# The recurrent block of layer one with its block-diagonal products behind the next tile's first product, and an out projection in half blocks

## The chip, the cores and the metric

The kernel runs on one core of a Trainium2 chip. The metric is the time of one execution on the device in microseconds (us), the median of several runs. The engines are called by the profile's names: PE is TensorE (PEld its weight loads), DVE is VectorE, ACT is ScalarE, POOL is GpSimd, and SP issues most of the DMAs.

## What is computed

The program is two blocks of a language model on 1024 tokens of width 1024, in float32. The first block has two layers: a recurrent layer ("hawk") with its feed-forward part, and an RWKV-7 layer with its own. The second block mixes a state-space layer and windowed attention. The change touches the recurrent layer alone. Cut to what matters it is:

```python
def hawk_block(x, w_in, b_in, conv_w, conv_b, wa, ba, wx, bx, lam, w_out, b_out):
    gx = x @ w_in + b_in                                  # 1024 -> 2 x 1280
    gate_branch, rec_branch = jnp.split(gx, 2, axis=-1)
    gate_branch = jax.nn.gelu(gate_branch)
    rec = causal_depthwise_conv(rec_branch, conv_w, conv_b)   # width 4
    rec = rg_lru(rec, wa, ba, wx, bx, lam)
    return (rec * gate_branch) @ w_out + b_out            # 1280 -> 1024

def rg_lru(x, wa, ba, wx, bx, lam):
    r = jax.nn.sigmoid(block_diag_linear(x, wa, ba))      # 10 blocks of 128 x 128
    i = jax.nn.sigmoid(block_diag_linear(x, wx, bx))
    log_a = -LRU_C * r * jax.nn.softplus(-lam)
    a = jnp.exp(log_a)
    b = jnp.sqrt(-jnp.expm1(2.0 * log_a)) * (i * x)
    ...  # h[t] = a[t] h[t-1] + b[t], along the tokens
    return h
```

## The kernel before, in words

Activations are held transposed, a channel tile of 128 rows by 512 tokens; the 1024 tokens are two halves. A float32 product is made from high and low fp32r parts: `mm3` (L191 to L193) issues three matmuls for each 128 rows of depth, high by high, high by low and low by high. So one output tile of depth 1024 is 24 matmuls. The weights come as a stream in a fixed order (class `Weights`): an SP load into one of two raw buffers, an ACT cast to the high part (L60, `whi`), a DVE difference for the low part (L65, `wlo`), into one of three split buffers. Products go to six rotating PSUM buffers (`mm`); two more (`aux`) serve small products.

The recurrent layer goes through ten channel tiles j of the inner width 1280, a step each, and then a step 10 without a new tile. In step j:

- `bd_gates(j-1)`: twelve matmuls, the two block-diagonal products of the tile before for both halves. They read `hxh` and `hxl`, the split conv output (L196 ACT, L197 DVE). ACT reads the four PSUM tiles (L414, L415: `hr`, `hi`), POOL multiplies (L416), ACT goes on to a tanh (L419).
- `rec(j, 0)`: the product of the recurrent branch for half 0 (24 matmuls, weight `hrec`); DVE takes it out of PSUM (L376, `hR`), makes the conv in four DVE operations (L379 once, L383 three times, `hX`), and splits it.
- `bd_decay(j-1)`: ACT exp and square (L424, L425), a DVE step (L426, `hb`), ACT square root (L429), a POOL product (L431).
- `rec(j, 1)`: the same for half 1.
- `bd_scan(j-1)` for each half: the recurrence as one DVE scan (L437), then POOL's product with the gate (L441).
- `gate(j)` for both halves: 48 matmuls with the weight `hgate`; DVE takes each out of PSUM (L394, `hG`), ACT makes the gelu (L395).
- `bd_split(j-1)`: the split of the gated result (`y`, L196 and L197).
- `outp`: in steps 3, 5, 7 and twice in 10 a block of two channel tiles goes through the out projection: 16 output tiles of six matmuls each, added to the residual `h` by DVE (L463/464 or L263). The last block also starts the next norm: an ACT and a DVE operation make the norm's split input (`hgh` L223, `hgl` L224), and ACT and POOL add squares.

The program order is that of the text above, but a scheduler with a model of the engines sets the order of each engine's instructions. It is a list for each engine; an instruction that waits holds up everything behind it on its engine. The feed-forward part that follows has the weight stream's next tiles, and the preparation of the second block (`s5_prep`, L1240 and on) is interleaved with it.

Of the kernel before, what the change touches and what calls it, by code (L numbers as in the profile page):

```python
# [28 lines left out]
class Weights:  # L29
    """Streams weight tiles in a fixed order: load, then split into two fp32r parts."""  # L30
# [23 lines left out]
    def _split(self, i):  # L54
# [6 lines left out]
        if kp < 128:                  # copies of 32 rows: (high, high, low) in one operand  # L61
            s = (slice(64, 96), s[1])
            self.nc.vector.tensor_tensor(out=hi[s], in0=t[s], in1=f32(hi[s]), op=SUB)
        else:
            self.nc.vector.tensor_tensor(out=lo[s], in0=t[s], in1=f32(hi[s]), op=SUB)  # L65
# [30 lines left out]
class Kernel:  # L96
# [4 lines left out]
    # ---------------------------------------------------------------- set-up  # L101
# [76 lines left out]
    # ------------------------------------------------------------ primitives  # L178
# [5 lines left out]
    def mm3(self, ps, w, x, nk, kofs=0, start=True, stop=True, kp=128, m=128):  # L184
        """ps += W^T x over nk row tiles; w = (hi, lo), x(k) -> (hi, lo)."""
# [13 lines left out]
    def split3(self, out, src, q):  # L199
        """out = three copies of 32 rows, high parts but for copy q, which has the low ones."""  # L200
# [4 lines left out]
    # norm whose 1/rms is applied after the product it feeds  # L205
# [6 lines left out]
    def norm_add(self, s, k, half, h=None):  # L212
        """h[k][half] is final: split gain*h, and add its squares."""
# [51 lines left out]
    # ----------------------------------------------------------------- start  # L265
    def load_x(self, yp):
        """x transposed to h, and its norm begun; x waits in tiles that the layer needs later."""
# [33 lines left out]
    # ------------------------------------------------------------------ hawk  # L301
    def hawk_weights(self):
# [3 lines left out]
        for j in range(10):  # L306
# [3 lines left out]
            for b in self.HB:  # L310
                if b[2] == j:
                    self._hawk_out_weights(w_out, b)
        for b in self.HB:
            if b[2] == 10:
                self._hawk_out_weights(w_out, b)

    def _hawk_out_weights(self, w_out, b):
        for q in range(2):
            self.W.add(("hout", b[0], q), [(0, 2, w_out[:, b[0]:b[1], q * 512:(q + 1) * 512])], 128, 2, 512)

    # channel tiles [a, b) go through the out projection after tile c's products
    HB = ((0, 2, 3), (2, 4, 5), (4, 6, 7), (6, 8, 10), (8, 10, 10))

    def hawk_consts(self, pool):
        """c = -8 softplus(-lambda), through log1p(u) = 2 atanh(u / (2 + u)), and the conv's bias."""
# [28 lines left out]
    def hawk(self, yp):  # L354
# [8 lines left out]
        def rec(j, half, w):  # L363
            p = self.psum()
# [5 lines left out]
            # the bias comes in with the conv's, so the padding is its negative  # L370
# [5 lines left out]
            tt(out=R[:, 3:], in0=p, in1=n0["rstd"][half], op=MUL)  # L376
            X = ht("hX", 2)
# [9 lines left out]
            st[j, half] = {"R": R, "X": X, "xs": (xh, xl)}  # L387
# [63 lines left out]
        def outp(b):  # L451
            a, e, _ = b
            last = e == 10
            for m in range(8):
                if m % 4 == 0:
                    wq = self.W.get(("hout", a, m // 4))
                w = tuple(t[:, :, (m % 4) * 128:(m % 4 + 1) * 128] for t in wq)
                for half in range(2):
                    p = self.psum()
                    self.mm3(p, w, lambda k: self.y[a + k, half], e - a)  # L460
                    self.run_deferred()
                    h = self.h[m, half]
                    if a == 0:  # L463
                        nc.vector.scalar_tensor_tensor(out=h, in0=p, scalar=self.v("lru_b_out", m), in1=h,
                                                       op0=ADD, op1=ADD)
                    else:
                        self.add_h(m, half, p)
# [1613 lines left out]
```

## Time and profile before

| | us |
|---|---|
| three runs | 3677.23, 3682.78, 3699.7 |
| their median | 3682.78 |
| the profiled execution, its span | 3682.5 |
| PE busy | 3477.9 (94% of the span) |
| DVE busy | 2453.6 (67%) |
| ACT busy | 1546.1 (42%) |
| POOL busy | 766.1 (21%) |

For the profiled execution nothing but its span is recorded, and the span lies 0.3 us under the median of the runs. The recurrent layer takes the first 465 us of the span. PE is the engine to look at: its idle time and the stretches at a lower granted clock are what a change of order can win. In the profile's timelines a row has its start, its length, the engine, the source line, the operation with output and inputs, how many rows it stands for, and in brackets the idle time ahead of it with what ended that.

### The profile page before, as it was taken

How to read it: one execution, taken by the hardware profiler on the slowest of the kernel's cores; microseconds unless marked ns; L12 is line 12 of the kernel's file. 1: busy time of each engine (PE TensorE's matmuls, PEld its weight loads, DVE VectorE, ACT ScalarE, POOL GpSimd, SP SyncE). 2: the span in 40 equal slices, each digit the busy share in tenths (PEclk: the TensorE clock that was granted, in tenths of full speed). 3: DMA queues.
4: the chain of work that ended last, by engine and by line, in shares of the span. 5: the costliest groups of instructions: out<-in, count | busy, mean ns of one | idle time of the engine just before them, and what ended most of it. 6: DMA issues, size and time to landing. Idle time of an engine off the chain costs nothing.

```text
span 3682.5 us, 49614 instructions
## 1 busy us (share of the span) xinstructions
PE 3477.9 (94%) x18603; PEld 2788.9 (76%) x18603; DVE 2453.6 (67%) x4254; ACT 1546.1 (42%) x2318; POOL 766.1 (21%) x1194
## 2 busy tenths in 40 slices
PE   7999899999999989999899899999999999799999
PEld 5777677777777867888678678887888888577777
DVE  7666778877675598467845985466544476886764
ACT  5665632223434452234444632334322254158553
POOL 4222358830210040012300410002000023240020
PEclk8999899999999989899899899999999999899999
DMA  3111113333443474732544646325323222121533
GB/s 98 42 41 38 35 47 94 106 107 110 119 124 118 134 214 110 163 91 80 171 123 143 199 135 157 100 70 152 92 83 112 64 86 85 55 90 49 184 90 113
DMA packets 626289, 388.86 MB, mean 106 GB/s; under 512 B 100212, under 2 KB 578208, under 8 KB 626048
## 3 DMA queue, kind: packets, MB, share of 16 engines
q1 hardware_dynamic: 619152, 373.07, 35.0%
q0 software_dynamic: 2944, 8.48, 0.7%
q10 hardware_dynamic: 3952, 4.13, 0.4%
q8 instruction: 147, 2.41, 0.3%
q14 instruction: 94, 0.77, 0.1%
HBM read 317.25 MB, written 68.35 MB: 105 GB/s over the span
## 4 chain that ended last, share of the span: by engine, by line
PE 43%; DVE 11%; DMA 3%; issue 3%; ACT 2%; SPq 1%; POOL 0%; DVEq 0%; ACTq 0%; POOLq 0%
PE mm L191 10%; PE mm L193 10%; PE mm L192 10%; DVE wlo L65 2%; PE g L1031 1%; DVE U L1562 1%; PE zy L1073 1%; PE g L1080 1%; PE zy L1070 1%; PE zy L1106 1%; DVE lnP L947 1%; PE mm L1773 1%; PE mm L1771 1%; PE mm L1772 1%; DVE lnT L949 1%
## 5 line engine op out<-in xcount | busy, mean ns | idle before, releaser
L191 PE MATMUL mm<-hgh,whi 128*128 128x512 f32 x2272 | 910.6, 401 | 13.4 <-DVE U L1562 9.9
L192 PE MATMUL mm<-hgl,whi 128*128 128x512 f32 x2272 | 904.6, 398 | 6.2 <-DVE hgl L224 6.2
L193 PE MATMUL mm<-hgh,wlo 128*128 128x512 f32 x2272 | 901.4, 397 | 5.2 <-DVE wlo L65 4.0
L60 ACT CAST whi<-wr 128x1024 fp32r<-128x1024 f32 (+3 forms) x566 | 478.4, 848 | 1014.4 <-PE mm L192 626.3
L65 DVE TENSOR_TENSOR wlo<-wr,whi 128x1024 fp32r<-128x1024 f32 (+3 forms) x564 | 571.3, 1014 | 290.7 <-ACT whi L60 271.1
L191 PEld LDWEIGHTS mm<-hgh,whi 128*128 128x128 f32 x2272 | 435.5, 192 | 114.6 <-issue 18.8
L193 PEld LDWEIGHTS mm<-hgh,wlo 128*128 128x128 f32 x2272 | 434.3, 191 | 102.8 <-DVE wlo L65 9.0
L192 PEld LDWEIGHTS mm<-hgl,whi 128*128 128x128 f32 x2272 | 435.3, 192 | 100.2 <-DVE hgl L224 7.5
L238 POOL TENSOR_TENSOR acc<-acc,sq 128x512 f32<-128x512 f32 x84 | 132.5, 1582 | 773.0 <-ACT sq L237 386.7
L193 PE MATMUL mm<-mh,wlo 128*128 128x512 f32 x704 | 277.0, 400 | 13.0 <-DVE wlo L65 12.3
L191 PE MATMUL mm<-mh,whi 128*128 128x512 f32 x704 | 279.0, 405 | 10.2 <-ACT whi L60 3.7
L192 PE MATMUL mm<-ml,whi 128*128 128x512 f32 x704 | 279.9, 398 | 1.6 <-DVE ml L197 1.5
L547 DVE TENSOR_TENSOR f<-mm,rstd 128x512 f32<-128x512 f32 x176 | 120.4, 685 | 235.6 <-PE mm L193 235.2
L263 DVE TENSOR_TENSOR h<-mm,h 128x512 f32<-128x512 f32 x272 | 182.3, 682 | 87.1 <-PE mm L193 86.4
L193 PEld LDWEIGHTS mm<-mh,wlo 128*128 128x128 f32 x704 | 134.5, 191 | 49.5 <-DVE wlo L65 20.5
L191 PEld LDWEIGHTS mm<-mh,whi 128*128 128x128 f32 x704 | 134.7, 192 | 47.9 <-ACT whi L60 9.5
L192 PEld LDWEIGHTS mm<-ml,whi 128*128 128x128 f32 x704 | 134.7, 191 | 30.2 <-DVE ml L197 3.2
L196 ACT CAST mh<-f 128x512 fp32r<-128x512 f32 x88 | 54.6, 621 | 199.4 <-DVE f L552 199.4
L880 POOL TENSOR_TENSOR t_s<-t_c,t_s 128x512 f32<-128x512 f32 x16 | 23.6, 1478 | 518.8 <-DVE t_c L878 518.8
L192 PE MATMUL mm<-xl,whi 128*128 128x512 f32 (+2 forms) x320 | 127.4, 400 | 0.0
L193 PE MATMUL mm<-xh,wlo 128*128 128x512 f32 (+2 forms) x320 | 126.9, 399 | 0.4 <-DVE wlo L65 0.3
L191 PE MATMUL mm<-xh,whi 128*128 128x512 f32 (+2 forms) x320 | 123.7, 398 | 3.4 <-DVE h L263 2.1
(617 smaller groups left out, 6294.2 us busy)
## 6 DMA issues: line engine op xcount, KB each, us to landing
wr<-in_ffn_w_in_dram SPq DMA_DIRECT2D x162, 512.0 KB, 3.8
wr<-in_ffn_w_out_dram SPq DMA_DIRECT2D x120, 256.0 KB, 2.8
wr<-in_rw_w_rkv_dram SPq DMA_DIRECT2D x48, 512.0 KB, 3.8
wr<-in_ple_w_gate_dram SPq DMA_DIRECT2D x24, 512.0 KB, 3.9
wr<-in_ffn_w_out_dram SPq DMA_DIRECT2D x56, 192.0 KB, 2.5
wr<-in_lru_w_in_dram SPq DMA_DIRECT2D x20, 512.0 KB, 3.8
wr<-in_w_in_dram SPq DMA_DIRECT2D x18, 512.0 KB, 4.4
hD<-h SPq DMA_DIRECT2D x32, 256.0 KB, 2.6
```

The source lines that it names most:

```text
L60: self.nc.scalar.copy(out=hi[s], in_=t[s])
L65: self.nc.vector.tensor_tensor(out=lo[s], in0=t[s], in1=f32(hi[s]), op=SUB)
L191: mm(ps, a, xh, start=start and k == 0, stop=False)
L192: mm(ps, a, xl, start=False, stop=False)
L193: mm(ps, b, xh, start=False, stop=stop and k == nk - 1)
L196: self.nc.scalar.copy(out=hi, in_=src)
L238: nc.gpsimd.tensor_tensor(out=a, in0=a, in1=q, op=ADD)
L263: self.nc.vector.tensor_tensor(out=h, in0=ps, in1=h, op=ADD)
L547: tt(out=t, in0=p, in1=nin["rstd"][half], op=MUL)
L947: nc.vector.tensor_tensor(out=p, in0=N[:, s, s + 1:32].unsqueeze(2).to_broadcast([128, r, c]), in1=X[:, s:s + 1, 0:c].to_broadcast([128, r ...
L949: nc.vector.tensor_tensor(out=X[:, s + 1:32, 0:c], in0=X[:, s + 1:32, 0:c], in1=p, op=ADD)
L1031: mm(p[e][:, q * 128:(q + 1) * 128], s["KB"][r, 4 * g + q, :], s["AR"][r, 4 * g + q, :], start=True, stop=True)
```

## The change

In step j the product of the recurrent branch for half 0 now stands ahead of the block-diagonal products of the tile before, so `rec` is cut into `rec_product` and `rec_conv`; the conv steps are issued after the products that follow on PE. The out projection's first three blocks are cut in two by output rows: after the gate products of steps 3 to 8 one half block of eight output tiles runs (one weight tile of 512 columns), where steps 3, 5 and 7 had sixteen. It now stands ahead of `bd_split`. The blocks of step 10 stand as (6, 8) before the last split and (8, 10) after it, and the last one goes by token halves: eight output tiles of half 0, its norm, then eight of half 1. Other hunks remove comments only; line numbers behind L300 move by up to 19.

```diff
@@ -307,22 +307,19 @@
             c = DR + j * 128
             W.add(("hrec", j), [(0, 8, w_in[:, :, c:c + 128])], 128, 8, 128)
             W.add(("hgate", j), [(0, 8, w_in[:, :, j * 128:(j + 1) * 128])], 128, 8, 128)
-            for b in self.HB:
-                if b[2] == j:
-                    self._hawk_out_weights(w_out, b)
-        for b in self.HB:
-            if b[2] == 10:
-                self._hawk_out_weights(w_out, b)
-
-    def _hawk_out_weights(self, w_out, b):
-        for q in range(2):
-            self.W.add(("hout", b[0], q), [(0, 2, w_out[:, b[0]:b[1], q * 512:(q + 1) * 512])], 128, 2, 512)
-
-    # channel tiles [a, b) go through the out projection after tile c's products
-    HB = ((0, 2, 3), (2, 4, 5), (4, 6, 7), (6, 8, 10), (8, 10, 10))
+            self._hawk_out_weights(w_out, j)
+        self._hawk_out_weights(w_out, 10)
+
+    def _hawk_out_weights(self, w_out, j):
+        for a, q in self.HO.get(j, ()):
+            self.W.add(("hout", a, q), [(0, 2, w_out[:, a:a + 2, q * 512:(q + 1) * 512])], 128, 2, 512)
+
+
+    HO = {3: ((0, 0),), 4: ((0, 1),), 5: ((2, 0),), 6: ((2, 1),), 7: ((4, 0),), 8: ((4, 1),),
+          10: ((6, 0), (6, 1), (8, 0), (8, 1))}
...
@@ -361,19 +358,27 @@
         st = {}
         self.y = {}
         def rec(j, half, w):
+            rec_product(j, half, w)
+            rec_conv(j, half)
+
+        def rec_product(j, half, w):
             p = self.psum()
             self.mm3(p, w, self.xof(n0, half), 8)
             self.run_deferred()
             if j == 0 and half == 0:
                 self.hawk_consts(yp)
             R = ht("hR", 2, n=HALF + 3)
+
             if half == 0:
                 nc.vector.tensor_scalar(out=R[:, 0:3], in0=self.ones[:, 0:3], scalar1=self.v("lru_b_in", 10 + j),
                                         scalar2=-1.0, op0=MUL, op1=MUL)
             else:
                 nc.vector.tensor_copy(out=R[:, 0:3], in_=st[j, 0]["R"][:, HALF:HALF + 3])
             tt(out=R[:, 3:], in0=p, in1=n0["rstd"][half], op=MUL)
+            st[j, half] = {"R": R}
+
+        def rec_conv(j, half):
+            R = st[j, half]["R"]
             X = ht("hX", 2)
             cw = self.vcol["lru_conv_w"]
             nc.vector.tensor_scalar(out=X, in0=R[:, 0:HALF], scalar1=self.vecs[:, cw + j:cw + j + 1],
@@ -384,7 +389,7 @@
                                                in1=X, op0=MUL, op1=ADD)
             xh, xl = ht("hxh", 2, F32R), ht("hxl", 2, F32R)
             self.split(xh, xl, X)
-            st[j, half] = {"R": R, "X": X, "xs": (xh, xl)}
+            st[j, half].update(X=X, xs=(xh, xl))
@@ -448,28 +453,35 @@
             self.split(yh, yl, st[j, half]["i"])
             self.y[j, half] = (yh, yl)
 
-        def outp(b):
-            a, e, _ = b
-            last = e == 10
-            for m in range(8):
-                if m % 4 == 0:
-                    wq = self.W.get(("hout", a, m // 4))
-                w = tuple(t[:, :, (m % 4) * 128:(m % 4 + 1) * 128] for t in wq)
+        def out_rows(a, m, half, w):
+
+            p = self.psum()
+            self.mm3(p, w, lambda k: self.y[a + k, half], 2)
+            self.run_deferred()
+            h = self.h[m, half]
+            if a == 0:
+                nc.vector.scalar_tensor_tensor(out=h, in0=p, scalar=self.v("lru_b_out", m), in1=h,
+                                               op0=ADD, op1=ADD)
+            else:
+                self.add_h(m, half, p)
+
+        def outp(a, q):
+            wq = self.W.get(("hout", a, q))
+            for m in range(4):
+                w = tuple(t[:, :, m * 128:(m + 1) * 128] for t in wq)
                 for half in range(2):
-                    p = self.psum()
-                    self.mm3(p, w, lambda k: self.y[a + k, half], e - a)
-                    self.run_deferred()
-                    h = self.h[m, half]
-                    if a == 0:
-                        nc.vector.scalar_tensor_tensor(out=h, in0=p, scalar=self.v("lru_b_out", m), in1=h,
-                                                       op0=ADD, op1=ADD)
-                    else:
-                        self.add_h(m, half, p)
-                    if last:
-                        self.norm_add(self.n1, m, half)
-                        if m == 7:
-                            self.norm_done(self.n1, half)
+                    out_rows(a, 4 * q + m, half, w)
                     yield
+
+        def out_last(a):
+            wq = [self.W.get(("hout", a, q)) for q in range(2)]
+            for half in range(2):
+                for m in range(8):
+                    w = tuple(t[:, :, (m % 4) * 128:(m % 4 + 1) * 128] for t in wq[m // 4])
+                    out_rows(a, m, half, w)
+                    self.norm_add(self.n1, m, half)
+                    yield
+                self.norm_done(self.n1, half)
 
@@ -478,7 +490,7 @@
             if j < 10:
                 w = self.W.get(("hrec", j))
             if j == 0:
...
@@ -486,13 +498,17 @@
                 rec(0, 1, w)
                 gate(0, 1, wg)
             if j:
+                if j < 10:
+                    rec_product(j, 0, w)
+                    yield
                 bd_gates(j - 1, wbd)
                 if j < 10:
-                    rec(j, 0, w)
+                    rec_conv(j, 0)
+                    rec_product(j, 1, w)
                 yield
                 bd_decay(j - 1)
                 if j < 10:
-                    rec(j, 1, w)
+                    rec_conv(j, 1)
                 yield
                 for half in range(2):
                     bd_scan(j - 1, half)
@@ -503,17 +519,20 @@
                 for half in range(2):
                     gate(j, half, w)
                     yield
+            if j < 10:
+                for a, q in self.HO.get(j, ()):
+                    yield from outp(a, q)
+            else:
+                self.n1 = self.norm_begin(self.hg, lambda k: self.v("norm_ffn", k))
+                yield from outp(6, 0)
+                yield from outp(6, 1)
             if j:
                 for half in range(2):
                     bd_split(j - 1, half)
-            for b in self.HB:
-                if b[2] == j:
-                    if b[1] == 10:
-                        self.n1 = self.norm_begin(self.hg, lambda k: self.v("norm_ffn", k))
-                    yield from outp(b)
-
-    # ------------------------------------------------------------------- ffn
-    # blocks of the inner width for one half at a time, then for both
+        yield from out_last(8)
+
```

In the built program the same operations stand on each engine, but for twelve ACT table loads fewer. Three places show what moved. In the names a number at the end tells buffers of one name apart.

First PE at step 3, where the block-diagonal products of tile 2 are taken up (`hxh_898` is half 0's operand, `hxh_945` half 1's; `mm_996` is the last gate product of step 2). Before:

```order
L193 MATMUL mm_996<-hgh_486,wlo_828 128x512
L191 MATMUL mm_1038<-hxh_898,wbh_958 128x512
L192 MATMUL mm_1038<-hxl_899,wbh_958 128x512
L193 MATMUL mm_1038<-hxh_898,wbl_959 128x512
L191 MATMUL mm_1039<-hxh_898,wbh_958 128x512
L192 MATMUL mm_1039<-hxl_899,wbh_958 128x512
L193 MATMUL mm_1039<-hxh_898,wbl_959 128x512
L191 MATMUL mm_1053<-hxh_945,wbh_958 128x512
L191 MATMUL mm_1054<-hxh_945,wbh_958 128x512
L191 MATMUL mm_1070<-hgh_184,whi_962 128x512
L192 MATMUL mm_1070<-hgl_185,whi_962 128x512
L192 MATMUL mm_1053<-hxl_946,wbh_958 128x512
```

In the change (`whi_962` is the weight of step 3's recurrent product):

```order
L191 MATMUL mm_1038<-hgh_285,whi_962 128x512
L192 MATMUL mm_1038<-hgl_286,whi_962 128x512
L193 MATMUL mm_1038<-hgh_285,wlo_963 128x512
L191 MATMUL mm_1066<-hxh_898,wbh_958 128x512
L192 MATMUL mm_1066<-hxl_899,wbh_958 128x512
L193 MATMUL mm_1066<-hxh_898,wbl_959 128x512
L191 MATMUL mm_1067<-hxh_898,wbh_958 128x512
L192 MATMUL mm_1067<-hxl_899,wbh_958 128x512
L193 MATMUL mm_1067<-hxh_898,wbl_959 128x512
L191 MATMUL mm_1081<-hxh_945,wbh_958 128x512
```

All 24 matmuls of `mm_1038`, the recurrent product of step 3, now stand between the gate product and the block-diagonal ones, and half 1's products come in one piece.

Second DVE in step 4, from the decay steps to the scans (`hb_1409` before and `hb_1367` in the change are the second half's). Before:

```order
L426 SCALAR_TENSOR_TENSOR hb_1409<-hr_1406,hb_1409 128x512
L376 TENSOR_TENSOR hR_1440<-mm_1415,rstd0_331 128x512
L437 SCALAR_TENSOR_TENSOR hi_1392<-ha_1393,hi_1392 128x512
L379 TENSOR_SCALAR hX_1443<-hR_1440,vecs_156,convb_334 128x512
L375 COPY hR_1487<-hR_1440 128x3
L440 COPY hH_1500<-hi_1392 128x1
L383 SCALAR_TENSOR_TENSOR hX_1443<-hR_1440,vecs_156,hX_1443 128x512
L437 SCALAR_TENSOR_TENSOR hi_1407<-ha_1408,hH_1500,hi_1407 128x512
L383 SCALAR_TENSOR_TENSOR hX_1443<-hR_1440,vecs_156,hX_1443 128x512 x2
L197 TENSOR_TENSOR y_1575<-hi_1392,y_1574 128x512
L372 TENSOR_SCALAR hR_1645<-ones_74,vecs_156 128x3
L376 TENSOR_TENSOR hR_1487<-mm_1462,rstd1_544 128x512
```

In the change:

```order
L388 SCALAR_TENSOR_TENSOR hX_1373<-hR_1338,vecs_156,hX_1373 128x512
L373 TENSOR_SCALAR hR_1613<-ones_74,vecs_156 128x3
L431 SCALAR_TENSOR_TENSOR hb_1367<-hr_1364,hb_1367 128x512
L377 TENSOR_TENSOR hR_1407<-mm_1382,rstd1_544 128x512
L197 TENSOR_TENSOR hxl_1379<-hX_1373,hxh_1378 128x512
L442 SCALAR_TENSOR_TENSOR hi_1350<-ha_1351,hi_1350 128x512
L384 TENSOR_SCALAR hX_1420<-hR_1407,vecs_156,convb_334 128x512
L65 TENSOR_TENSOR wlo_1505<-wr_1311,whi_1504 128x1024
L445 COPY hH_1430<-hi_1350 128x1
L388 SCALAR_TENSOR_TENSOR hX_1420<-hR_1407,vecs_156,hX_1420 128x512
L442 SCALAR_TENSOR_TENSOR hi_1365<-ha_1366,hH_1430,hi_1365 128x512
L388 SCALAR_TENSOR_TENSOR hX_1420<-hR_1407,vecs_156,hX_1420 128x512
```

The first half's take-out `hR` and its conv (`hX_1443` before, `hX_1373` in the change) stand ahead of the second `hb` now and not behind it, and the two `y` splits are gone from between the scans and the gates' take-outs `hG`; they stand behind seven of the half block's eight additions.

Third DVE in the last block of the out projection (`h_114` to `h_121` are half 0's residual tiles, `h_125` to `h_132` half 1's), at the split of the feed-forward part's second weight tile, `wlo_3367`. Before:

```order
L263 TENSOR_TENSOR h_117<-mm_3177,h_117 128x512
L224 SCALAR_TENSOR_TENSOR hgl_3171<-h_127,vecs_156,hgh_3170 128x512
L263 TENSOR_TENSOR h_128<-mm_3192,h_128 128x512
L224 SCALAR_TENSOR_TENSOR hgl_3186<-h_117,vecs_156,hgh_3185 128x512
L263 TENSOR_TENSOR h_118<-mm_3213,h_118 128x512
L65 TENSOR_TENSOR wlo_3367<-wr_3087,whi_3366 128x1024
L224 SCALAR_TENSOR_TENSOR hgl_3201<-h_128,vecs_156,hgh_3200 128x512
```

In the change:

```order
L263 TENSOR_TENSOR h_127<-mm_3248,h_127 128x512
L224 SCALAR_TENSOR_TENSOR hgl_3242<-h_126,vecs_156,hgh_3241 128x512
L263 TENSOR_TENSOR h_128<-mm_3263,h_128 128x512
L224 SCALAR_TENSOR_TENSOR hgl_3257<-h_127,vecs_156,hgh_3256 128x512
L263 TENSOR_TENSOR h_129<-mm_3278,h_129 128x512
L65 TENSOR_TENSOR wlo_3367<-wr_3087,whi_3366 128x1024
L224 SCALAR_TENSOR_TENSOR hgl_3272<-h_128,vecs_156,hgh_3271 128x512
L263 TENSOR_TENSOR h_130<-mm_3293,h_130 128x512
```

The split stands behind the addition for the thirteenth output tile now (`h_129`), and stood behind the ninth (`h_118`).

## Rows read from the trace of the kernel before

**Rows 1.** Windows, PE: span; stretch, width, busy us (matmuls), clock, DMA share, GB/s.

```profile
core 0 of [0], span 3682.5 us
50.00:81.00 31.00, 21.12 (x76) 0.78 0.14 39
110.00:135.00 25.00, 18.48 (x61) 0.73 0.15 42
150.00:404.00 254.00, 229.80 (x956) 0.95 0.13 40
404.00:430.00 26.00, 17.88 (x56) 0.74 0.13 41
465.00:490.00 25.00, 18.83 (x67) 0.86 0.15 27
50.00:500.00 450.00, 394.87 (x1592) 0.92 0.13 39
166.00:203.00 37.00, 37.00 (x164) 1.00 0.15 47
```

**Rows 2.** Waits of PE, first 480 us: line, released by, us in total, times, longest.

```profile
PE mm L191 <- ACT hxh L196: 23.5, 12, 6.6
...
PE mm L191 <- DVE hG L394: 8.6, 6, 2.9
```

**Rows 3.** Timeline of PE in the recurrent layer and behind it.

```profile
59.66 0.80 PE L192 MATMUL mm<-hxl,wbh 128*128 128x512 f32 x1 [2.52 <-DVE hxl L197]
...
68.34 0.79 PE L191 MATMUL mm<-hxh,wbh 128*128 128x512 f32 x1 [6.61 <-ACT hxh L196]
...
179.55 0.39 PE L191 MATMUL mm<-hxh,wbh 128*128 128x512 f32 x1
...
212.81 0.63 PE L191 MATMUL mm<-hgh,whi 128*128 128x512 f32 x1
...
213.24 0.63 PE L192 MATMUL mm<-hxl,wbh 128*128 128x512 f32 x1
...
465.75 0.39 PE L191 MATMUL mm<-hgh,whi 128*128 128x512 f32 x1
...
484.41 0.80 PE L192 MATMUL mm<-hgl,whi 128*128 128x512 f32 x1 [5.18 <-DVE hgl L224]
```

**Rows 4.** Timeline of DVE in step 4.

```profile
194.37 1.43 DVE L426 SCALAR_TENSOR_TENSOR hb<-hr,hb 128x512 f32<-128x512 f32 x1 [3.68 <-ACT hr L425]
...
195.72 0.68 DVE L376 TENSOR_TENSOR hR<-mm,rstd 128x512 f32<-128x512 f32 x1
...
197.45 1.45 DVE L379 TENSOR_SCALAR hX<-hR,vecs,convb 128x512 f32<-128x512 f32 x1
...
198.95 0.73 DVE L383 SCALAR_TENSOR_TENSOR hX<-hR,vecs,hX 128x512 f32<-128x512 f32 x1
...
201.83 2.42 DVE L383 SCALAR_TENSOR_TENSOR hX<-hR,vecs,hX 128x512 f32<-128x512 f32 x2
...
204.18 0.68 DVE L197 TENSOR_TENSOR y<-hi,y 128x512 fp32r<-128x512 f32 x1
...
209.75 0.68 DVE L394 TENSOR_TENSOR hG<-mm,rstd 128x512 f32<-128x512 f32 x1
...
212.38 0.68 DVE L394 TENSOR_TENSOR hG<-mm,rstd 128x512 f32<-128x512 f32 x1
```

**Rows 5.** Timeline of DVE in and behind the last block.

```profile
456.82 1.19 DVE L224 SCALAR_TENSOR_TENSOR hgl<-h,vecs,hgh 128x512 fp32r<-128x512 f32 x1
...
458.54 1.72 DVE L65 TENSOR_TENSOR wlo<-wr,whi 128x1024 fp32r<-128x1024 f32 x1
...
483.52 0.17 DVE L1240 TENSOR_SCALAR ae<-st 128x16 f32<-128x16 f32 x1 [6.21 <-DMA st<-in_ssm_log_step_dram]
```

**Rows 6.** Timeline of SP's queue behind the last block.

```profile
461.33 1.43 SPq L1326 DMA_DIRECT2D st<-in_ssm_log_step_dram  x2
...
483.98 0.38 SPq L1314 DMA_DIRECT2D lraw<-in_ssm_lam_im_dram  x1
```

## The prediction

> **What bounds the kernel now.** I read the windows of PE first [rows 1]. In the undisturbed stretch 166 to 203, 164 matmuls take 37.00 us, 0.226 each; no order can make them faster. So the width of a stretch less 0.226 for each of its matmuls is what waits and a lower clock cost there, and I call it the excess. For 50 to 500 it is 450 - 1592 x 0.226 = 90 us, all that a new order of the recurrent layer can win, 2.4% of the span. By place it is 13.8 in 50 to 81 (step 1), 11.2 in 110 to 135 (step 3's block-diagonal products), 37.9 in 150 to 404 (the out block of step 3 up to step 9), 13.3 in 404 to 430 (step 10) and 9.9 in 465 to 490 (behind the last block). The sum of waits by cause comes next [rows 2]: 23.5 us in twelve waits for `hxh`, the conv output that the block-diagonal products read, and 8.6 in six waits for `hG`, the DVE operation that takes a gate product out of PSUM. The timelines show where they lie and what follows [rows 3]: behind the waits of step 5 matmuls start 0.43 us apart (212.81, 213.24), nearly twice 0.226, so PE is granted its lower level there. At step 1 the two waits of 2.52 and 6.61 leave 4.7 of the excess of 13.8, for two stretches at that level and smaller waits; I take 2.2 us for one stretch.
>
> **The change, part by part.** The operations stay the same, so the sum is the excess of each place, before less after. T is the start of a block-diagonal product on PE. A recurrent or gate product is 24 x 0.226 = 5.4 us, the block-diagonal ones 2.7, an output tile of six matmuls 1.36.
>
> Step 1. The recurrent product now runs first, so half 0's low part, which came at 59.66, is needed only about 61 and costs no wait. Half 1's operand came at 68.34 [rows 3] and is needed at about 62.5; its conv is a little earlier on DVE, so 5.0 to 5.8 us stay, and 2.2 of clock: 7.9. Gain 13.8 - 7.9 = 5.9 (bounds 4 and 9).
>
> Step 3. From the block-diagonal products of step 2 to those of step 3 PE has 24.5 us of work in both orders, but half 0's conv now stands on DVE ahead of the decay steps, so half 1's operand comes earlier. I find it about T + 26 by the sum below, against 24.5 and the 1.7 us that `wlo` of the next recurrent weight will hold PE, plus 1.36 for half 0's products: no further wait. Excess 1.8 for 11.2, gain 9.4 (bounds 6 and 11).
>
> Steps 3 to 9. Between two block-diagonal products lie 35 us of PE work now, in steps 4 to 9 alike, where it was 46 and 25 in turn, and half 1's operand comes about T + 26, so the waits for `hxh` in steps 5, 7 and 9 vanish. What takes their place are the six half blocks. With six PSUM buffers in turn, the fifth output tile needs the buffer of the first gate product, the sixth that of the second. PE reaches the fifth at T + 2.7 + 5.4 + 10.8 + 4 x 1.36 = T + 24.4 and the sixth at T + 25.8. When DVE has read them I take from step 4 of the trace, where T is 179.55 [rows 3] and nothing waited: its second decay step `hb` starts at 194.37, T + 14.8, and what sets that (four sigmoids, tanh, exp on ACT) keeps its order. The gate products were read from 209.75 and 212.38, 15.4 and 18.0 behind `hb` [rows 4]. Of the work between, six things stand elsewhere in the new order: the first half's take-out 0.68, its conv 1.45 + 0.73 + 2.42 and two `y` splits of 0.68, less 0.08 by which a row starts before the last one's end in each of six, 6.2 together. So the reads start at T + 24.0 and T + 26.6 and end 0.7 later. The fifth tile waits 0.3; the sixth, then due at T + 26.1, waits 1.2; the seventh needs the first tile's addition, behind a `wlo` split on DVE, and waits about 0.5. POOL's second gate product lies beside the last conv steps and stretches them by some 0.4. That is 2.4 a half block, 14.4 in six (a mean wait for `hG` is 1.4 in before [rows 2]). With 2 us of small excess that I leave, 16.4 stand for 37.9, gain 21.5. The bounds are none and 5 us for each half block (0 and 30). The added weight waits are nothing: the same tiles come in the same stream, one for each half block, with 10.8 us of PE work to cover each.
>
> The Trainium skill speaks against this part: "Perfetto Trace Analysis", section Identifying Performance Opportunities, says that the same gap repeating on the engine that should be saturated can mean that PSUM lacks room for the next tile. The trace agrees, with the six waits for `hG` in three blocks [rows 2]. By that rule the 8.6 us would double with the six half blocks, to 17.2, and the forecast would be 2.8 us later.
>
> Step 10. The products of tile 9 follow the gate products of step 9 without a recurrent product or a half block between, so half 1's operand, about T + 26.4, is needed at T + 20.4: 6.0, with 2.7 of clock, and PSUM waits of 4. 12.7 for 13.3, gain 0.6 (bounds -4 and 3).
>
> Behind the last block. Before, PE began the feed-forward part at 465.75 and waited 5.18 for `hgl` until 484.41 [rows 3]. That `hgl` stood on DVE behind a 6.21 us wait for the load of `st` [rows 5], a load that SP issued at 461.33 [rows 6], behind the next weight load, which waits until `wlo` (458.54, 1.72 long) has freed a raw buffer. In the new order that `wlo` stands behind four more additions and four more `hgl`; a pair takes 1.72 (456.82 to 458.54) [rows 5]. It ends some 6.9 us later, and so do SP's loads. `st` lands about 490 then, and the second `lraw`, issued at 483.98 [rows 6] and now without a weight load shortly ahead of it, is issued about 490; its transpose stands on PE ahead of the rest. PE has 50 matmuls, 11.3 us, behind the last block, to about 477, and waits to about 491: 14 of wait, 2.2 of clock and 1 of small excess, 17.2 for 9.9. A loss of 7.3 (bounds 0 and 9). Half 0's earlier norm gains nothing while this wait ends last.
>
> The sum: 5.9 + 9.4 + 21.5 + 0.6 - 7.3 = 30.1 us. Against the profiled span of 3682.5 that is 3652.4; the span is 0.3 under the median of the runs, so the forecast is **3653 us**, 0.8% faster.
>
> **The rivals.** A difference under 1% (36.8 us, so above 3646 and under 3719.6) cannot be told from no change here.
>
> (a) The half blocks meet no wait: DVE, rid of the first half's conv and the `y` splits at the critical place, reads both gate products 2 us sooner than I find. Then the 14.4 go too: 3638. For it speaks that the reads lie within 2 us of the need; against it the waits for `hG` in all three blocks of before.
>
> (b) Dearer block waits. Either the lower clock follows each wait, as it did behind the step 5 waits of under 2.1 us: 6 x 2.2 = 13 more, 3666. Or POOL's operations hold DVE longer than I count: beside POOL two conv steps took 2.42 where one alone took 0.73 [rows 4], so 0.96 more. Two further such meetings between `hb` and the second read give 1.9 a step, 11.5 in six: 3664. Both: 3677. Against the clock speaks that the half blocks' waits are short and broken by 1.36 us of work. The Trainium skill, "SBUF — State Buffer", section Who interferes with whom, says that a DVE operation with two SBUF inputs and a GpSimd operation that reads SBUF exclude each other, the later one blocked fully. The 2.42 agrees; by that rule the second case of (b) holds wherever the two lists meet.
>
> (c) Slower than before: the first half's conv now stands ahead of the decay steps on DVE, and its buffer `hX` is one that POOL must have read. If that holds DVE, the decay steps, scans and reads of the gates come as late as before, the second read ending at T + 33.5 (213.06 less 179.55) [rows 3, 4]. Each sixth tile then waits 7.7 and the clock falls: 9.9 for 2.4, 45 us in six, 3697. It decides from 7.4 us of excess a half block. Against it: POOL is free before the decay steps need DVE, by about 2 us in step 4.
>
> (d) The change does nothing because the scheduler puts the old order back: the order of PE and DVE above excludes it.
>
> **How the numbers follow.** The forecast, 3643 to 3662, gets 0.50; (a) 0.22; (b) 0.20; (c) 0.07; something larger on the slow side 0.01. Faster by over 1% takes (a) and the lower edge of the forecast with a better tail, 0.34; slower by over 1% would need more than (c): 0.03; within 1% 0.63. The range 3630 to 3676 leaves out (c), the far ends of (a) and of (b), about 0.2.
>
> **What would show it.** In the windows of PE by step: about 8 us of excess in step 1, no wait for `hxh` in steps 2 to 9, and waits for `hG` or the first addition at the fifth to seventh tile of each half block, 2.4 together at a clock of 1.00. Behind the last block a wait of some 14 us, its end set by `st` or `lraw`. The forecast is wrong if `hb` comes later than T + 15, if the block-diagonal products still wait in odd steps, or if the tail's wait stays near 5.

## The result and the profile after

The changed kernel runs in 3645.75 us, median of four runs (3632.09 to 3649.95), against 3682.9 for the kernel before on the same chip: a ratio of 0.9894, 95% interval 0.9868 to 0.992, so 37 us or 1.1% faster. The forecast was 3653 with a range of 3630 to 3676. A second set of runs, together with experiments, gave 3649.5 and 0.9905 (0.9891 to 0.9919).

The page of the profiled execution (3649.95 us, its span 1.85 less) has these lines:

```profile
span 3648.1 us, 49644 instructions
...
PE 3454.9 (95%) x18603; PEld 2775.5 (76%) x18603; DVE 2452.3 (67%) x4254; ACT 1529.4 (42%) x2306; POOL 760.1 (21%) x1194
```

The span is 34.4 us shorter than before, and PE is busy 23 us less with the same 18603 matmuls. Of that, 19 us lie ahead of the transposes of the input `p` (948.66 before, 916.78 now), the first work behind the first feed-forward part; the mean granted clock up to there was 0.95 and is 0.97 now. The windows of PE that answer to [rows 1] follow (stretch, width, busy us and matmuls, clock, DMA share, GB/s); the steps begin earlier now, so the borders have moved:

```profile
50.00:81.00 31.00, 26.11 (x102) 0.89 0.14 39
103.00:135.00 32.00, 31.39 (x138) 1.00 0.14 39
135.00:360.00 225.00, 213.23 (x924) 1.00 0.15 46
360.00:400.00 40.00, 30.59 (x124) 0.91 0.09 27
430.00:460.00 30.00, 15.64 (x57) 0.72 0.19 40
```

By the same reckoning, width less 0.226 for each matmul, the excess is 7.9 in step 1 (13.8 before), 0.8 up to step 3's half block (11.2), 16.2 in the half blocks and steps to 9 (37.9), 12.0 in step 10 (13.3) and 17.1 behind the last block (9.9). That is 54.0 for 86.1, a gain of 32.1. The waits of PE up to 480 us answer to [rows 2]:

```profile
PE aux L1335 <- DMA lraw<-in_ssm_lam_im_dram: 14.4, 1, 14.4
...
PE mm L191 <- DVE hG L399: 11.2, 7, 2.5
...
PE mm L191 <- ACT hxh L196: 10.2, 2, 5.3
...
PE mm L192 <- DVE hxl L197: 0.6, 1, 0.6
```

The waits for `hxh` fell from 23.5 us in twelve to 10.2 in two, step 1's and step 10's. With them went those for `hxl`, the low part of the same operand, which were the second longest group before:

```profile
PE mm L192 <- DVE hxl L197: 14.0, 6, 2.7
```

The waits for `hG` rose from 8.6 us in six to 11.2 in seven, and one new wait leads the list: 14.4 us for the load of the second `lraw`. Three rows of PE's timeline in step 4, that wait, and the first of the transposes of `p`:

```profile
160.21 0.39 PE L191 MATMUL mm<-hxh,wbh 128*128 128x512 f32 x1
...
179.30 0.39 PE L191 MATMUL mm<-y,whi 128*128 128x512 f32 x1
...
187.48 0.50 PE L191 MATMUL mm<-y,whi 128*128 128x512 f32 x1 [1.22 <-DVE hG L399]
...
453.02 0.28 PE L1335 MATMUL aux<-ident,lraw 16*128 16x16 f32 x1 [14.36 <-DMA lraw<-in_ssm_lam_im_dram]
...
916.78 0.48 PE L602 MATMUL mm<-ident,pin 128*128 128x128 f32 x1 [4.50 <-DMA pin<-in_p_dram]
```

DVE's timeline in steps 3 (its first row) and 4, and behind the last block:

```profile
135.93 1.43 DVE L431 SCALAR_TENSOR_TENSOR hb<-hr,hb 128x512 f32<-128x512 f32 x1 [2.50 <-ACT hr L430]
...
163.98 0.55 DVE L384 TENSOR_SCALAR hX<-hR,vecs,convb 128x512 f32<-128x512 f32 x1 [2.68 <-POOL hi L421]
...
173.70 1.43 DVE L431 SCALAR_TENSOR_TENSOR hb<-hr,hb 128x512 f32<-128x512 f32 x1 [2.49 <-ACT hr L430]
...
176.26 2.31 DVE L442 TENSOR_TENSOR_SCAN hi<-ha,hi 128x512 f32<-128x512 f32 x1
...
183.66 0.68 DVE L399 TENSOR_TENSOR hG<-mm,rstd 128x512 f32<-128x512 f32 x1
...
186.74 0.68 DVE L399 TENSOR_TENSOR hG<-mm,rstd 128x512 f32<-128x512 f32 x1
...
426.58 2.12 DVE L65 TENSOR_TENSOR wlo<-wr,whi 128x1024 fp32r<-128x1024 f32 x1
...
451.25 0.17 DVE L1259 TENSOR_SCALAR ae<-st 128x16 f32<-128x16 f32 x1 [11.97 <-DMA st<-in_ssm_log_step_dram]
```

In the kernel before, the scan of step 4 that stands at 176.26 here was this row, 1.1 us shorter:

```profile
196.31 1.21 DVE L437 TENSOR_TENSOR_SCAN hi<-ha,hi 128x512 f32<-128x512 f32 x1
```

With T at 160.21 the first tile of the half block starts at T + 19.1, the second `hb` at T + 13.5, the gate products are read from T + 23.5 and T + 26.5, and the tile that waits for the second read stops PE for 1.22 us. The first conv operation waited 2.68 for POOL, and that wait was over before `hb` was due. Half 1's operand is cast by ACT until 186.10, T + 25.9:

```profile
185.48 0.62 ACT L196 CAST hxh<-hX 128x512 fp32r<-128x512 f32 x1 [0.38 <-DVE hX L388]
```

And SP's queue behind the last block:

```profile
429.77 1.43 SPq L1345 DMA_DIRECT2D st<-in_ssm_log_step_dram  x2
...
431.25 7.52 SPq L1393 DMA_DIRECT2D br<-in_ssm_b_re_dram  x2
...
438.81 5.89 SPq L1393 DMA_DIRECT2D bi<-in_ssm_b_im_dram  x2
...
447.71 0.37 SPq L1333 DMA_DIRECT2D lraw<-in_ssm_lam_im_dram  x1
```

The loads of `br` and `bi` that follow `st`, two of each, hold the queue for 13.4 us, and `lraw` is issued behind them and two more loads.

In the kernels below PE executes the same 3615 matmuls ahead of the transposes of `p` and the same 14988 from there on. So the start of the transposes of `p` (916.78 here, 948.66 before) divides each profile into a front, where the recurrent layer lies, and a rest.

| kernel | median us | ratio to before, 95% | front | rest of the span |
|---|---|---|---|---|
| before | 3683 to 3691 | | 948.7 | 2733.8 |
| the change | 3645.75 | 0.9868 to 0.992 | 916.8 | 2731.3 |
| the change again (e5_after) | 3649.5 | 0.9891 to 0.9919 | 916.1 | 2729.2 |
| first part alone (e1_bd) | 3658.6 | 0.9921 to 0.9945 | 916.7 | 2740.7 |
| first part undone, last block by rows (e2_half) | 3670.6 | 0.9949 to 0.9976 | 932.2 | 2733.8 |
| last block by rows (e3_mlast) | 3650.2 | 0.9893 to 0.992 | 909.2 | 2739.6 |
| the same again (e5_mlast) | 3638.2 | 0.9851 to 0.9895 | 910.5 | 2725.2 |
| `st` loaded early (e4_early) | 3677.9 | 0.9971 to 0.9994 | 924.9 | 2751.3 |
| `st` as rows (e6_st) | 3632.7 | 0.9847 to 0.9874 | 903.6 | 2731.8 |
| two tiles in aux (e7_aux) | 3637.0 | 0.9853 to 0.9883 | 906.8 | 2731.5 |
| both remedies (e8_all) | 3617.9 | 0.9781 to 0.9819 | 888.7 | 2728.5 |
| both, last block by rows (e8m_all) | 3630.2 | 0.9811 to 0.9848 | 892.7 | 2737.3 |

### The profile page after: what moved, and what is told of

Same layout as the page of the kernel before. It is cut to its first block, busy times and chain, and to the rows that moved or that the text cites. A ratio compares the mean times of both kernels' runs of the same rounds, so it can differ in the third digit from the quotient of the medians.

```text
span 3648.1 us, 49644 instructions
## 1 busy us (share of the span) xinstructions
PE 3454.9 (95%) x18603; PEld 2775.5 (76%) x18603; DVE 2452.3 (67%) x4254; ACT 1529.4 (42%) x2306; POOL 760.1 (21%) x1194
## 5 line engine op out<-in xcount | busy, mean ns | idle before, releaser
L193 PE MATMUL mm<-mh,wlo 128*128 128x512 f32 x704 | 277.8, 401 | 13.3 <-DVE wlo L65 12.6
```

Source lines behind the costliest of these rows:

```text
L193: mm(ps, b, xh, start=False, stop=stop and k == nk - 1)
```

## Experiments

**e1_bd: the first part alone.**

```diff
 # the kernel before, with rec cut into rec_product and rec_conv
+                if j < 10:
+                    rec_product(j, 0, w)
+                    yield
                 bd_gates(j - 1, wbd)
                 if j < 10:
-                    rec(j, 0, w)
+                    rec_conv(j, 0)
+                    rec_product(j, 1, w)
 ...
```

> The kernel before with the first part of the change alone: the recurrent product of half 0 ahead of the block-diagonal products, whole out blocks after steps 3, 5 and 7 and the last block as before. Theory (each part acts where it stands): step 1 falls to 8 us of excess and step 3 to 1 us as in the change, a gain of 16 us; in steps 5, 7 and 9 the half-1 operand still comes about T + 26 and is needed at T + 24.4 + 1.4, so at most a short wait stays there (1 us each for 7 to 8 before), a gain of some 20; the whole blocks keep their waits of 3 to 4 us each; behind the last block nothing changes (10 us). 3647 us, within 4 of the change. Rival (the half blocks are what lets the operand come in time): steps 5, 7 and 9 keep 7 to 8 us each, 3667 us.

Measured 3658.6 us. Five rows of its PE timeline:

```profile
197.27 0.50 PE L192 MATMUL mm<-hxl,wbh 128*128 128x512 f32 x1 [0.61 <-DVE hxl L197]
...
223.05 0.80 PE L191 MATMUL mm<-y,whi 128*128 128x512 f32 x1 [2.57 <-DVE hG L402]
...
226.53 0.50 PE L191 MATMUL mm<-y,whi 128*128 128x512 f32 x1 [0.56 <-DVE hG L402]
...
380.98 1.22 PE L191 MATMUL mm<-hxh,wbh 128*128 128x512 f32 x2 [8.34 <-ACT hxh L196]
...
452.24 0.79 PE L192 MATMUL mm<-hgl,whi 128*128 128x512 f32 x1 [5.14 <-DVE hgl L224]
```

In step 5 (197.27) 0.61 us is left of the wait for the operand, and steps 7 and 9 are alike: the theory holds, and the half blocks aren't what lets the operand come in time. The whole block of step 5 waits for both gate products (223.05, 226.53), step 10 waits 8.34 where the change waits 5.27, and behind the last block 5.14 stays as before. The front ends at 916.7, the same as with the whole change. Of the 12 us by which the median misses the expected time, 9 lie behind the front (2740.7 for the change's 2731.3), where PE runs the same operations in the same order of tile names.

**e2_half: the first part undone, and with it the token halves of the last block.**

```diff
 # the change
         def out_last(a):
-            for half in range(2):
-                for m in range(8):
+            for m in range(8):
+                for half in range(2):
 ...
-                if j < 10:
-                    rec_product(j, 0, w)
-                    yield
                 bd_gates(j - 1, wbd)
                 if j < 10:
-                    rec_conv(j, 0)
-                    rec_product(j, 1, w)
+                    rec(j, 0, w)
 ...
```

> The change with its first part undone: block-diagonal products ahead of the recurrent product again, half blocks after steps 3 to 8, the last block by token halves. Theory: step 1 14 us and step 3 11 us of excess as before, +16 us against the change; from step 4 on each step has a half block, 30 us of work from T to the next block-diagonal product against an operand at T + 32 or so, waits of 2 to 5 us at each of steps 4 to 9 and with them the lower clock, +20; 3680 us, as before the change. Rival (half blocks alone suffice because they even out the steps): no waits from step 4 on, 3662 us.

What ran is not quite what was expected: the edit also puts the last block back to output rows, so the kernel to compare it with is that of the next experiment, e3_mlast, and not the change. Measured 3670.6 us. Rows of PE in steps 1 and 4 and behind the last block:

```profile
69.13 0.79 PE L191 MATMUL mm<-hxh,wbh 128*128 128x512 f32 x1 [6.61 <-ACT hxh L196]
...
200.35 0.50 PE L191 MATMUL mm<-y,whi 128*128 128x512 f32 x1 [0.61 <-DVE hG L399]
...
205.30 0.50 PE L191 MATMUL mm<-y,whi 128*128 128x512 f32 x1 [1.91 <-DVE h L463]
...
468.74 0.79 PE L192 MATMUL mm<-hgl,whi 128*128 128x512 f32 x1 [5.82 <-DVE hgl L224]
```

Step 1 keeps its wait of 6.61 and step 3 its waits, as the theory said, but from step 4 to 9 no operand is late: the rival is right there, and the 30 us of work that the theory counted between two block-diagonal products were a slip, since it is 35 whichever product stands first. Either part alone takes the odd steps' waits away, all but 0.6 us. Each half block waits 1.8 to 2.5 us here (0.61 and 1.91 in step 4). Beside the half blocks, with the last block by rows in both, the first part is worth 21.7 to 23.0 us of front (932.2 less the 910.5 and 909.2 of that kernel's two profiles), and 20.4 by the medians of one chip.

**e3_mlast and e5_mlast: the last block by output rows.**

```diff
-            for half in range(2):
-                for m in range(8):
+            for m in range(8):
+                for half in range(2):
 ...
```

> The change with its third part undone: the last block by output rows, both halves of a row in turn, as before. Theory (the token halves delay a weight split on DVE by four additions and four norm splits, and with it the loads of the second block's parameters): the wait behind the last block goes back from 14.4 us for the second lraw to about 5 us for the norm split, excess there 10 for 17, 3639 us. Rival (the loads are late whatever the order, or the early norm of half 0 is worth as much as the wait): no difference, 3646 us.

Measured 3650.2 us, and in this profile the wait behind the last block is back at what it was:

```profile
444.84 0.80 PE L192 MATMUL mm<-hgl,whi 128*128 128x512 f32 x1 [5.32 <-DVE hgl L224]
```

The front is 7.6 us shorter than the change's, as the theory says, and yet the median is not. So the pair was run again, both on one chip.

> The changed kernel itself again, beside the three that follow on the same chip, as the measure for them: 3646 us. The wait of 14.4 us for lraw stands behind the last block again and the waits of the half blocks at 1.2 to 1.6 us each; behind 920 us the time to the end varies from execution to execution with the granted clock (2731 us in its first profile).

> The change with the last block by output rows again. Its profile had the front 7.5 us earlier at 917 us and lost 8 us behind it, where not one instruction of PE differs but 65 places of its order. Theory (the loss behind 917 us is the granted clock's, which differs between executions): beside the change on one chip it is 4 to 8 us faster, 3640 us. Rival (the loss belongs to this kernel's order): same as the change or 3 to 5 slower, 3650 us.

Now 3649.5 and 3638.2. The front is 5.6 us shorter by rows; the rest is 4.0 shorter, where in the first pair it was 8.3 longer. The same program has a rest of 2739.6 and of 2725.2 us in its two profiles, which come from two chips, and PE is busy for 2623.5 and 2609.4 of it: the difference lies in how long the same matmuls took, and not in waits. On one chip the five runs of e5_mlast lie between 3624.9 and 3648.3. Where that shows is the RWKV stretch. There PE is busy without a gap; its window of 1500 to 1600 in the change:

```profile
1500.00:1600.00 100.00, 100.00 (x1040) 0.98 0.34 95
```

in e3_mlast:

```profile
1500.00:1600.00 100.00, 100.00 (x952) 0.86 0.31 85
```

and in e5_mlast, which is the same program:

```profile
1500.00:1600.00 100.00, 100.00 (x952) 0.91 0.32 89
```

One order of instructions was granted 0.86 in one execution and 0.91 in the other. So a difference of some 10 us between two medians here can come from the rest alone; the front repeats within 1.4 us. By the front, the last block by token halves costs 5.6 to 7.6 us.

**e4_early: `st` loaded early.**

```diff
+    def s5_loads(self):                       # called at step 4
+        self.s5st = self.const.tile([128, 16], F32, name="st")
+        for g in range(2):
+            nc.scalar.dma_start(out=self.s5st[g * 64:(g + 1) * 64, :], in_=ls[:, g, :].to_broadcast([64, 16]))
 ...
-            raw = tp.tile([16, 128], F32, tag="lraw", name="lraw", bufs=1)
+            raw = tp.tile([16, 128], F32, tag="lraw", name="lraw", bufs=3)
```

> The change with the parameter st of the second block loaded early, through ACT's queue into a tile of its own, and three buffers for lraw instead of one, so that its second load does not stand behind the first one's use. Theory (the 14.4 us wait is these two loads' alone): the wait goes, with the lower clock behind it, excess behind the last block 1 to 3 us for 17, 3631 us; half 0's early norm then counts. Rival (the next late operand, the last norm splits on DVE or the second weight, takes its place): excess 8 to 12, 3638 to 3642 us. A cost of the early load at the start of the program would show in the first 50 us.

Measured 3677.9 us, 32 slower than the change. Rows of its PE timeline:

```profile
29.27 0.45 PE L289 MATMUL mm<-ident,xt 128*128 128x128 f32 x1 [12.42 <-DMA xt<-in_x_dram]
...
33.96 0.47 PE L289 MATMUL mm<-ident,xt 128*128 128x128 f32 x1 [4.24 <-DMA xt<-in_x_dram]
...
458.22 0.50 PE L192 MATMUL mm<-hgl,whi 128*128 128x512 f32 x1 [0.92 <-DVE hgl L224]
```

The wait behind the last block is 0.92 us, so it was these two loads' alone, those of `st` and `lraw`. But the scheduler put the load where its tile was free, at the start of the program. The queues of ACT and SP there:

```profile
9.48 0.70 ACTq L1331 DMA_DIRECT2D st<-in_ssm_log_step_dram  x1
...
9.54 9.28 SPq L281 DMA_DIRECT2D xt<-in_x_dram  x3
```

SP's issue of the three loads of `x` took 9.28 us, where the change's took 3.33, and `x` came 12.4 and 4.2 us late. The first norm's sum on PE comes 16.2 us later than in the change, of which the front has got back half.

That is not all of the 32 us: 20 of them lie in the rest, 2751.3 for 2731.3, and all eleven runs lie between 3670 and 3684. In many stretches PE's matmuls lie further apart, at the same granted clock. The same 400 of them, in the change and in e4_early:

```profile
2606.90:2698.16 91.26, 91.12 (x401) 1.00 0.36 104
...
2624.92:2718.13 93.21, 93.08 (x401) 1.00 0.35 102
```

No other run here shows that, and why this one does stays open. So the placing of the load explains the late start and not the whole loss, and the median of e4_early doesn't tell what the remedy is worth.

**e6_st: `st` as rows.**

```diff
-        for g in range(2):
-            nc.sync.dma_start(out=st[g * 64:(g + 1) * 64, :], in_=ls[:, g, :].to_broadcast([64, 16]))
+        srow = tp.tile([128, 32], F32, name="srow")
+        nc.sync.dma_start(out=srow, in_=i["ssm_log_step_2"].to_broadcast([128, 32]))
+        sv = srow.rearrange("r (p g) -> r g p", g=2)
+        for g in range(2):
+            r = slice(g * 64, (g + 1) * 64)
+            nc.vector.tensor_copy(out=st[r, :], in_=sv[r, g, :])
 # and three lraw buffers, as above
```

> The change with the parameter st loaded as one row of 32 for each partition (128 packets of 128 bytes) and picked apart by two DVE copies, where before 2048 single elements of 4 bytes are loaded, and with three buffers for lraw. Theory (the single elements make the load slow, 21 us, and the one buffer puts the second lraw behind everything): both land within 5 us, the wait of 14.4 us goes and the clock behind it stays up, 15 to 17 us faster than the change, 3630 us, and the first 50 us as in the change. Rival (the queue of SP is what is slow, whatever is in it): the wait stays at 8 to 14 us, 3640 to 3646 us.

Measured 3632.7 us, 17 under the change on the same chip. The DMA view behind the last block (output and input, engine and operation, count, KB each, median us from issue to landing), of the change:

```profile
st<-in_ssm_log_step_dram SPq DMA_DIRECT2D x2, 4.0 KB, 20.7
br<-in_ssm_b_re_dram SPq DMA_DIRECT2D x2, 16.0 KB, 15.7
bi<-in_ssm_b_im_dram SPq DMA_DIRECT2D x2, 16.0 KB, 10.1
```

and of e6_st:

```profile
br<-in_ssm_b_re_dram SPq DMA_DIRECT2D x2, 16.0 KB, 2.5
bi<-in_ssm_b_im_dram SPq DMA_DIRECT2D x2, 16.0 KB, 2.1
```

The next load, 16 KB of `br`, lands in 2.5 us, where behind the old `st` it took 15.7. The slow thing was not SP's queue but the 2048 elements that stood in it. The edit has two parts, `st` as rows and three `lraw` buffers, that were not run apart. In the change DVE had `st` at 451.25, and only behind that came the `hgl` that PE needs next, so three buffers alone could have shortened the wait, which ended at 453.02, by some 2 us at most; whether `st` as rows alone would do is not shown. Of the 14.4 us wait this is left:

```profile
441.85 0.50 PE L192 MATMUL mm<-hgl,whi 128*128 128x512 f32 x1 [1.55 <-DVE hgl L224]
```

The Trainium skill, "DMA: Bandwidth & Descriptors", section Rules for kernel authors, says that a strided last dimension becomes one descriptor for each element and should be made contiguous. The trace agrees: with the two loads of `st` among ACT's (e4_early), their queue, q10, moved 2288 packets in the first 50 us, and without them (the change) 208, so 2080 more for 2048 elements.

**e7_aux: two tiles of each half block in the aux buffers.**

```diff
-        def out_rows(a, m, half, w):
-            p = self.psum()
+        def out_rows(a, m, half, w, aux=False):
+            p = self.aux() if aux else self.psum()
 ...
-                    out_rows(a, 4 * q + m, half, w)
+                    out_rows(a, 4 * q + m, half, w, a < 6 and m == 2)
```

> The change with the fifth and sixth output tile of each half block in the two other PSUM buffers (aux), which are idle there. Theory (those tiles wait because DVE has not read the gate products whose buffers they take): the waits for hG in steps 3 to 8, 11.2 us together, fall under 2 us, the two of step 3 included, 8 to 11 us faster than the change, 3636 us. Rival (what is late is DVE, and the tiles behind wait in their place for the additions or the next step's operand): the same sum under other names, 3646 us.

Measured 3637.0 us, 12 under the change. Its waits for `hG`:

```profile
PE mm L191 <- DVE hG L399: 1.9, 1, 1.9
```

11.2 us in seven waits became 1.9 in one, in step 3, and nothing took their place. The half blocks waited for PSUM buffers that DVE had not read.

**e8_all and e8m_all: both remedies.** Their edits are those of e6_st and e7_aux together, the second with the loops of e3_mlast.

> The change with both remedies: st as rows and three lraw buffers, and the fifth and sixth output tile of each half block in the aux buffers; the last block by token halves. Theory (the two waits lie at different places and their gains add): 17 and 12 us under the change's 3649, 3620 us. Rival (with the half blocks' waits gone the next step's operand or the granted clock takes a part back): 3626 to 3632 us.

> The same two remedies, with the last block by output rows. Theory (with the loads in time the order of the last block no longer sets the load of st, but by rows both halves' last norm splits come at the end): same as with token halves or up to 3 us slower, 3620 to 3623 us. Rival (token halves cost by DVE's order, not by the loads alone): 3614 us.

Measured 3617.9 us (ratio 0.98, 0.9781 to 0.9819) and 3630.2. Neither remedy takes from the other: by the medians they gave 16.8 and 12.5 us alone and 31.7 together, though this pair ran on another chip, where the kernel before took 3690.7 for 3683.9; by the front 12.5, 9.3 and 27.4, which is 5.6 more than the sum, and the runs do not show why. e8_all beats both kernels, by 2.0% the one before and by 28 to 32 us the change. e8m_all is 12.3 us slower, where its theory had up to 3 and its rival a gain. With the loads in time the token halves gain 4.0 us of front; the other 8 lie in the rest, where one program's profiles differ by 14, and are not shown to be theirs.

## Why the prediction held

The forecast said 30.1 us of gain; the profile shows 34.4, of which 31.9 lie in the front and 2.5 in the rest, where nothing was forecast and two profiles of one program differ by 14. The median is 7 us under the forecast.

- **Step 1**: 7.9 us of excess forecast, 7.9 measured. Half 1's operand is late by 4.9 us, where 5.0 to 5.8 were forecast, and the clock and what else is lost take 3.1, where 2.2 were.
- **Step 3**: 1.8 forecast, 0.8 measured. No `wlo` held PE; 0.61 for `hxl` did.
- **Steps 3 to 9**: 16.4 forecast, 16.2 measured: the mechanism is the forecast's, but that the numbers agree to 0.2 is luck. Half 1's operand came at T + 25.9 (forecast 26), the waits for `hxh` are gone, and six half blocks wait for the gates' reads, at the clock of 1.00. These waits are 11.2 us, not 14.4 (nor the 17.2 of before's waits doubled), and the small excess beside them is 5.0, not 2. In steps 4 to 8 it is one wait of 1.2 to 1.6 a half block where three with 2.4 together were forecast. In step 4 `hb` came at T + 13.5 and not T + 14.8, and from there to the reads DVE took 10.0 and 13.0 us, not 9.2 and 11.8: the scan lies beside a POOL product that began 0.3 us ahead of it and takes 2.31 us, where it began first before and took 1.21. The two misses nearly cancel, the reads come at T + 23.5 and T + 26.5 (forecast 24.0 and 26.6), so the fifth tile didn't wait and the sixth waited the 1.2 of the sum. Step 3 waits 2.53 and 1.82: with T at 118.31, its `hb` comes at T + 17.6, past the T + 15 that was named as a sign of a wrong forecast, and two `y` splits stand ahead of its second read still, as they do in steps 5 and 7, where the wait is the 1.6. The sum was made for step 4 and carried over to all six.
- **Step 10**: 12.7 forecast, 12.0 measured, with a wait of 5.27 for `hxh` where 6.0 was forecast.
- **Behind the last block**: 17.2 forecast, 17.1 measured. The wait is 14.4 against 14, and it ends with `lraw`. That the loads follow the `wlo` split is shown by e3_mlast, that they are nearly the whole wait by e4_early and e6_st (0.92 and 1.55 are left). What the forecast did not name is why `st` is slow.

Of the rivals, (a) was excluded by the waits for `hG`; e7_aux shows what it would have been worth, 9 us by the front and 12 by the medians. (b) failed in its first half: no lower clock followed the waits of 1.2 to 2.5 us. Its second half was true in part: of the two further meetings with POOL that it priced one came, the scan's, at 1.1 us a step, and only because `hb` came 1.3 us earlier were the gate products of steps 4 to 8 read no more than 0.3 us later than summed. (c) failed because the conv's wait for POOL, 2.68 us on DVE in step 4, ended at T + 3.8, long before `hb` at T + 13.5.

The forecast gave within 1% the larger chance, and the median came out at 1.1%, on the border.

The gain was booked to parts wrongly in one respect. The sum gave the 21.5 us of steps 3 to 9 to the two moves together. e1_bd has the front of the whole change, 916.7, with the first part alone, and e2_half takes the same odd steps' waits away with the half blocks alone. With the last block by rows, the first part alone shortens the front by 32.0 us, the half blocks with step 10's new order by 16.4, and both by 38.1 to 39.5 (910.5 and 909.2): they share 9 to 10. So the half blocks add 6.1 to 7.5 us to the first part, and the token halves take them back.

## What to carry to other kernels

Before moving work, write for each wait when its operand comes and how much work lies ahead of it in the new order, from one start T, and count what is moved on the slower engine too; here that gave five places within 1 us each, in part by misses that cancelled. A sum made for one step is to be made again for a step whose order differs. Where the pieces of a block wait for shared buffers, ask which idle buffers could take them: two gave 9 to 12 us here. A load on the path after a reordering is to be looked at by its packets, not by its bytes: 8 KB of single elements held up nearly all of a wait of 14 us here, and the loads behind them in the queue came late as well.

## What the runs showed of the hardware

Two loads of 4 KB in single elements took 20.7 us to land, and the loads of 16 KB behind them took 15.7 and 10.1 in place of 2.5 and 2.1. On another engine's queue, at the start of the program, they delayed the loads of SP's queue: `x` came 12.4 and 4.2 us late (e4_early).

A DVE scan of 128x512 that began 0.3 us behind a POOL product took 2.31 us (176.26 in the change); one that began 0.3 us ahead of such a product took 1.21 (196.31 before), and the product 2.01 instead of 1.54.

Seven waits of PE between 1.2 and 2.5 us, two of them 3.5 us apart in step 3 and the others some 37, left the granted clock at 1.00 in 135 to 360. Behind the three waits of step 5 before, 1.6 to 2.1 us each within 8 us, matmuls started 0.43 us apart [rows 3], the lower level.

Code that runs without a gap on PE, in one and the same order, was granted 0.86 and 0.91 in two executions on two chips, and the rest of the span differed by 14 us. What sets that wasn't tried; runs of that program on one chip differ by 23 us.
